# GpSimd instead of VectorE subtracts the lower parts of 24 split weight blocks in layer 3

## The chip, the cores and the metric

The kernel runs on one core of a Trainium2 chip. The metric is the device time of one execution in microseconds (us); several executions are timed and the median is taken. One further execution is recorded by the hardware profiler, and the rows below come from it. Engines are named as in the profile: PE is TensorE, PEld its weight loads, DVE is VectorE, ACT is ScalarE, POOL is GpSimd, SP is SyncE.

## The reference

The program is a trunk of four layers over 256 latent tokens and 256 context tokens, 1024 wide. Each layer has a token mixer and a squared-ReLU MLP, with a modulated input and a LayerNorm behind each. The fourth layer (number 3) mixes with a gated delta rule, and this is the layer that the change touches:

```python
def project(t):
    qkv, z, b_f, b_b, a_f, a_b = jnp.split(t @ w_in, cuts, axis=-1)
    qkv = jax.nn.silu(_centred_dwconv(qkv, conv_w))
    q, k, v = jnp.split(qkv, _cuts(GDN_KEY_DIM, GDN_KEY_DIM), axis=-1)
    q = jnp.repeat(_l2_norm(_heads(q, GDN_KEY_HEADS)), rep, axis=1) * GDN_HEAD_DIM ** -0.5
    k = jnp.repeat(_l2_norm(_heads(k, GDN_KEY_HEADS)), rep, axis=1)
    v = _heads(v, GDN_VALUE_HEADS)
...
t_inv = lax.linalg.triangular_solve(lmat, eye, left_side=True, lower=True, unit_diagonal=True)
u_vals = t_inv @ (v * beta[..., None])
...
def step(s, inp):
    u_c, w_c, q_c, a_c, k_c, d_c = inp
    v_new = u_c - w_c @ s
    o = q_c @ s + a_c @ v_new
    s = s * d_c[..., None, None] + jnp.swapaxes(k_c, -1, -2) @ v_new
    return s, o
```

There are 8 key heads and 16 value heads of 128 columns each; the sequences are cut into chunks of 64 tokens, and one triangular system is solved for each chunk and value head, in both directions.

## The kernel before

Activations lie transposed: 128 features on the partitions, tokens along the free axis. A weight block is 128 x 1024 numbers, 512 KB: 8 tiles of 128 x 128, one for each 128 of the 1024 inputs. Most products are made in three passes of a faster 32-bit format. The weight w is split into a rounded upper part `whi` and the rest `wlo = w - whi`, the activation likewise into `uh` and `ul`, and `mm3` adds three products: `ul` by `whi` (L296), `uh` by `whi` (L297), `uh` by `wlo` (L298). Queries and gates of layer 3 (`gdn_q`, `gdn_z`) are not split; they are multiplied whole in 32 bits (L1546).

For every split block `halved` does three things: SP loads it into a `raw` buffer (L271, four of them), ACT rounds it into `whi` (L279), DVE subtracts (L280) and writes `wlo`. `whi` and `wlo` have rings of four buffers. `weights` fetches two blocks ahead of the product that takes them.

Layer 3 begins in `gdn_products`. A list of jobs (`GDN_JOBS`) sets the order of the queries, keys, values and gates; beside them runs `gdn_solve`, twice, once for each group of four key heads. A key or value block gives 24 products of 512 columns in PSUM (`acc` or `pj`). Then `conv` makes a five-tap convolution: one instruction on ACT (L1389) and four on DVE (L1392), each reading the product from PSUM and the running sum `y` from SBUF. A value then goes through ACT (L233), four transposes on PE (L1587), ACT again (L1590), and POOL issues the DMA that spills it to HBM (L1591); POOL also issues the DMAs of gates (L1598) and of the solve's results (L1421, L1483).

`gdn_solve` builds its matrices on DVE from `side`, `kk` and `kq` (L1410 to L1420), transposes 32 x 32 blocks on DVE (L1441), eliminates with alternating products and differences of two SBUF tiles on DVE (L1446 and L1448), transposes back (L1452, L1453), and joins blocks by small products on PE (L1462, L1478) with copies on DVE and ACT (L1471, L1480). POOL clears tiles with memsets (L1431, L1472).

After that come the scans over chunks (`gdn_scans`), the output product and the last MLP. A scheduler lays all instructions of the program into one fixed order for each engine, from its own costs, when the program is built. Each engine works through its queue in that order, and so does SP with its DMAs.

Of the kernel before, what the change touches and what calls it, by code (L numbers as in the profile page):

```python
# [12 lines left out]
F32 = mybir.dt.float32  # L13
# [22 lines left out]
GDN_BANKS = dict(accs=3, st=3, ax=2)  # L36
GDN_PLAN = (0, 0.5, 0.4), (0, 0.6, 0.75)
GDN_JOBS = "q0 k1 q1 v v v z z z v v v z z v v z v z v v z z v v z z z z v v z v".split()
TABLES = "natural_log_exp_and_others"
GDN_ROWS = dict(y=3, x=2, v=2, side=3)  # L40
ADA_SUMS = 1
# [116 lines left out]
class Trunk:  # L158
    def __init__(self, ctx, tc, ins, out):
# [12 lines left out]
        self.wraw, self.wsplit = pool("wraw", 4), pool("wsplit", 4)  # L172
        nc.scalar.preload_act_table_set(TABLES)
        c = self.const
# [62 lines left out]
    def tables(self):  # L237

        if self.silued is not None:
            self.loaded = self.after(self.nc.scalar.preload_act_table_set(TABLES), self.silued)  # L240
            self.silued = None
# [17 lines left out]
    def load(self, name, *at):  # L259

        src = self.I[name]
        for j in at:
            src = src[j]
        if name in ("gdn_q", "gdn_z"):
            return self.whole(src)
        last = name == "mla_in" and at[0] in (4, 5) or name in ("mla_out", "diff_out", "gla_out") and at[0] >= 4 or name == "w2" and at[1] >= 4 and at[2] == 3
        return self.halved(self.tail if last else self.wsplit, src)

    def whole(self, src):
        raw = self.wraw.tile([128, 1024], F32, name="raw")  # L270
        self.nc.sync.dma_start(raw[:, :src.shape[-1]], src)  # L271
        return raw

    def halved(self, pool, src, n=""):

        nc, width = self.nc, src.shape[-1]
        raw = self.whole(src)
        hi, lo = (pool.tile([128, 1024], F32R, name=m + n) for m in ("whi", "wlo"))
        nc.scalar.copy(hi[:, :width], raw[:, :width])  # L279
        nc.vector.tensor_sub(lo[:, :width], raw[:, :width], hi[:, :width].bitcast(F32))  # L280
        return hi, lo

    def blocks(self):
# [466 lines left out]

    gdn_jobs = GDN_JOBS

# [1189 lines left out]
```

## Time and profile before

| what | value |
|---|---|
| median of 3 timed executions | 2735.97 us (2731.73 to 2740.79) |
| the profiled execution: its time | 2734.95 us |
| the profiled execution: its span | 2733.2 us |
| PE busy | 2630.0 us (96%) |
| DVE busy | 2007.7 us (73%) |
| ACT busy | 1251.6 us (46%) |
| POOL busy | 46.2 us (2%) |
| all subtractions on L280, 403 of them | 477.9 us of DVE |

The span is what the profiler's rows cover; 1.75 us of the execution's time lie around it. Busy is the time in which an engine has at least one instruction in work; for PE the ends of matmuls are modelled and run into one another, so that a busy PE isn't a PE at its peak. Layer 3's keys, values, gates and solves lie between 2007 and 2290 us of the span.

### The profile page before, as it was taken

To read this page: it belongs to the slowest core of one execution; us is meant where nothing else is said; L and a number is where in the kernel's file an instruction comes from. 1 tells how busy PE (TensorE), PEld (TensorE's weight loads), DVE (VectorE), ACT (ScalarE), POOL (GpSimd) and SP (SyncE) were. 2 spreads that over 40 slices of the span, in tenths; PEclk is the share of its full clock that TensorE was granted. 3 is DMA by queue.
4 is the path that set the end of the run, shared out by engine and by line. 5 is a ranking of instruction groups with operands and counts; after the bars stand their busy time and mean duration, and the time that the engine had idled before them with its cause. 6 is when DMAs were issued, how large, how long until landed. Compare 5 with 4: busy or idle time off the path is not lost. (4 is left out here: it accounts for less than half of the span.)

```text
span 2733.2 us, 40942 instructions
## 1 busy us (share of the span) xinstructions
PE 2630.0 (96%) x15728; PEld 2137.2 (78%) x15728; DVE 2007.7 (73%) x3796; ACT 1251.6 (46%) x2413; POOL 46.2 (2%) x71
## 2 busy tenths in 40 slices
PE   7999999999999999999999999999999998997998
PEld 5666888888866687888888897888887776667997
DVE  3577898775667798775745489876689996679666
ACT  3555453234556653333445553332464545445544
POOL 0000000000000000000000000000000111000000
PEclk9999999999999999999999999999999998999999
DMA  6533246553221137554221127654323445304453
GB/s 237 169 121 111 68 155 207 185 185 118 65 64 54 47 100 225 191 184 131 73 70 62 55 70 226 195 181 153 104 85 105 160 151 157 90 28 139 155 183 111
DMA packets 125535, 353.25 MB, mean 129 GB/s; under 512 B 37499, under 2 KB 41339, under 8 KB 124828
## 3 DMA queue, kind: packets, MB, share of 16 engines
q1 hardware_dynamic: 121804, 337.00, 38.8%
q0 software_dynamic: 3536, 13.63, 1.4%
q8 instruction: 124, 2.03, 0.3%
q14 instruction: 71, 0.58, 0.1%
HBM read 335.91 MB, written 14.68 MB: 128 GB/s over the span
## 5 line engine op out<-in xcount | busy, mean ns | idle before, releaser
L279 ACT CAST whi<-raw 128x1024 fp32r<-128x1024 f32 (+2 forms) x403 | 410.7, 1024 | 681.6 <-PE acc L297 244.9
L280 DVE TENSOR_TENSOR wlo<-raw,whi 128x1024 fp32r<-128x1024 f32 (+2 forms) x403 | 477.9, 1189 | 209.5 <-ACT whi L279 197.5
L296 PE MATMUL pj<-ul,whi 128*128 128x512 f32 (+1 forms) x1072 | 395.1, 369 | 0.1
L297 PE MATMUL pj<-uh,whi 128*128 128x512 f32 (+1 forms) x1072 | 385.2, 359 | 0.0
L298 PE MATMUL pj<-uh,wlo 128*128 128x512 f32 (+1 forms) x1072 | 383.8, 358 | 0.7 <-DVE wlo L280 0.5
L452 DVE SCALAR_TENSOR_TENSOR acc<-raw,s,acc 128x1024 f32<-128x1024 f32 x252 | 317.2, 1280 | 34.9 <-DMA raw<-in_ada 31.6
L296 PE MATMUL acc<-ul,whi 128*128 128x512 f32 (+3 forms) x888 | 312.5, 352 | 17.6 <-DVE ul L568 10.7
L297 PE MATMUL acc<-uh,whi 128*128 128x512 f32 (+3 forms) x888 | 309.8, 349 | 0.0
L298 PE MATMUL acc<-uh,wlo 128*128 128x512 f32 (+3 forms) x888 | 308.5, 348 | 0.1
L296 PEld LDWEIGHTS pj<-ul,whi 128*128 128x128 f32 x1072 | 204.0, 190 | 36.4 <-issue 6.1
L298 PEld LDWEIGHTS pj<-uh,wlo 128*128 128x128 f32 x1072 | 203.5, 190 | 34.6 <-issue 5.4
L297 PEld LDWEIGHTS pj<-uh,whi 128*128 128x128 f32 x1072 | 203.8, 190 | 29.4 <-issue 5.2
L296 PEld LDWEIGHTS acc<-ul,whi 128*128 128x128 f32 (+2 forms) x888 | 168.6, 190 | 42.3 <-DVE ul L568 12.7
L296 PE MATMUL pj<-hl,whi 128*128 128x512 f32 (+1 forms) x560 | 196.5, 351 | 1.7 <-DVE hl L635 1.3
L297 PE MATMUL acc<-hh,whi 128*128 128x512 f32 (+1 forms) x560 | 195.4, 349 | 0.0
L297 PE MATMUL pj<-hh,whi 128*128 128x512 f32 (+1 forms) x560 | 194.8, 348 | 0.0
L296 PE MATMUL acc<-hl,whi 128*128 128x512 f32 (+1 forms) x560 | 194.8, 348 | 0.0
L298 PE MATMUL acc<-hh,wlo 128*128 128x512 f32 (+1 forms) x560 | 194.7, 348 | 0.0
L298 PE MATMUL pj<-hh,wlo 128*128 128x512 f32 (+1 forms) x560 | 194.2, 347 | 0.0
L298 PEld LDWEIGHTS acc<-uh,wlo 128*128 128x128 f32 (+2 forms) x888 | 168.4, 190 | 21.8 <-issue 1.0
L297 PEld LDWEIGHTS acc<-uh,whi 128*128 128x128 f32 (+2 forms) x888 | 168.5, 190 | 20.9 <-issue 1.2
L634 ACT CAST hh<-t 128x512 fp32r<-128x512 f32 (+1 forms) x128 | 72.2, 567 | 129.7 <-DVE t L633 129.3
(463 smaller groups left out, 4887.2 us busy)
## 6 DMA issues: line engine op xcount, KB each, us to landing
raw<-in_w SPq DMA_DIRECT2D x256, 512.0 KB, 4.2
raw<-in_ada SPq DMA_DIRECT2D x192, 512.0 KB, 4.7
raw<-in_diff_qk SPq DMA_DIRECT2D x16, 512.0 KB, 3.4
raw<-in_gdn_v SPq DMA_DIRECT2D x16, 512.0 KB, 4.0
raw<-in_gdn_z SPq DMA_DIRECT2D x16, 512.0 KB, 4.0
raw<-in_gdn_out SPq DMA_DIRECT2D x16, 512.0 KB, 3.9
raw<-in_mla_in SPq DMA_DIRECT2D x9, 512.0 KB, 7.0
raw<-in_mla_qb SPq DMA_DIRECT2D x12, 384.0 KB, 3.8
```

The source lines that it names most:

```text
L279: nc.scalar.copy(hi[:, :width], raw[:, :width])
L280: nc.vector.tensor_sub(lo[:, :width], raw[:, :width], hi[:, :width].bitcast(F32))
L296: mm(ps, lhsT=ah, rhs=bl, start=start, stop=False)
L297: mm(ps, lhsT=ah, rhs=bh, start=False, stop=False)
L298: mm(ps, lhsT=al, rhs=bh, start=False, stop=stop)
L452: nc.vector.scalar_tensor_tensor(acc[r], w, self.s[:, k, r:r + 1], acc[r], op0=ALU.mult, op1=ALU.add)
L634: nc.scalar.copy(hh[:, f, :t], r[:, :t])
```

## The change

Two names are put into a table, and blocks of these names have their subtraction on POOL. `whi` stays with ACT, the DMA with SP, the arithmetic is the same.

```diff
+LOW_APART = "gdn_k", "gdn_v"
...
-        return self.halved(self.tail if last else self.wsplit, src)
+        return self.halved(self.tail if last else self.wsplit, src, low=self.nc.gpsimd if name in LOW_APART else None)
...
-    def halved(self, pool, src, n=""):
+    def halved(self, pool, src, n="", low=None):
...
-        nc.vector.tensor_sub(lo[:, :width], raw[:, :width], hi[:, :width].bitcast(F32))
+        (low or nc.vector).tensor_sub(lo[:, :width], raw[:, :width], hi[:, :width].bitcast(F32))
```

8 blocks of keys and 16 of values are concerned: 24 instructions leave DVE's queue and 24 enter POOL's. The scheduler then lays the layer out anew. After the change every line number above 38 is higher by 2.

The first place is POOL's queue where the first solve ends: `xc` and `xa` are tiles of the solve, `uc` its spilled result, `at` a spilled result of the second solve's start, `v` and `z` spilled values and gates. Before:

```order
L1598 DMA z_17226<-s 128x256
L1472 MEMSET xc 32x32x32 x2
L1472 MEMSET xa 32x32x32 x2
L1483 DMA uc_17231<-xc 128x2048
L1483 DMA uc_17233<-xa 128x2048
L1431 MEMSET xc 128x2048
L1433 MEMSET xc 128x32 x2
L1421 DMA at_17236<-side 128x512 x2
L1421 DMA at_17238<-side 128x512 x2
```

The same place of the changed kernel:

```order
L282 TENSOR_TENSOR wlo<-raw,whi 128x1024
L1474 MEMSET xc 32x32x32 x2
L1474 MEMSET xa 32x32x32 x2
L1485 DMA uc_17231<-xc 128x2048
L1600 DMA z_17226<-s 128x256
L1485 DMA uc_17233<-xa 128x2048
L1433 MEMSET xc 128x2048
L1435 MEMSET xc 128x32 x2
L282 TENSOR_TENSOR wlo<-raw,whi 128x1024
L1423 DMA at_17236<-side 128x512 x2
L282 TENSOR_TENSOR wlo<-raw,whi 128x1024
L1423 DMA at_17238<-side 128x512
```

Subtractions of value blocks now stand between POOL's memsets and spills, and start only after those ahead of them; the two first here are those of value heads 9 and 10 (counted from 0), and that of head 10 stands behind both `uc` spills and the memset of L1431.

The second place is PE's queue at the same point of the program: L1546 is a gate's product, L296 to L298 are those of a value block, L1587 transposes a value, L1462 the first joining products of the first solve. Before:

```order
L1587 MATMUL ax<-ident,x 128x128 x4
L1546 MATMUL pj<-u,raw 128x256 x2
L296 MATMUL acc<-ul,whi 128x512
L297 MATMUL acc<-uh,whi 128x512
L298 MATMUL acc<-uh,wlo 128x512
...
L296 MATMUL acc<-ul,whi 128x512
L1462 MATMUL st<-xa,lo 32x32 x64
L297 MATMUL acc<-uh,whi 128x512
```

The same place of the changed kernel:

```order
L1589 MATMUL ax<-ident,x 128x128 x4
L1548 MATMUL pj<-u,raw 128x256 x3
L1464 MATMUL st<-xa,lo 32x32 x64
L1548 MATMUL pj<-u,raw 128x256 x2
L298 MATMUL acc<-ul,whi 128x512
L1464 MATMUL st<-xa,lo 32x32 x64
L299 MATMUL acc<-uh,whi 128x512
```

Before, 34 products of value blocks (the dots leave out 30 of the same three kinds) stood between the gate's products and the first 64 joining products. Now the joining products stand ahead of these 34, so that PE reaches them earlier.

## Rows read from the trace of the kernel before

**Rows 1.** Busy time by stretch: length, then engines' busy us (instructions), PEclk, DMA share, GB/s.
```profile
1930.00:2010.00 80.00, 78.03 (x523) 71.10 (x521) 61.66 (x138) 40.42 (x79) 3.03 (x4) 1.00 0.28 88
2010.00:2085.00 75.00, 68.73 (x366) 53.15 (x367) 70.01 (x141) 40.29 (x76) 2.55 (x4) 0.98 0.33 106
2085.00:2135.00 50.00, 49.12 (x223) 40.41 (x222) 49.15 (x88) 20.52 (x49) 4.51 (x7) 0.99 0.42 135
2135.00:2210.00 75.00, 69.25 (x841) 53.76 (x840) 68.41 (x110) 46.92 (x88) 14.99 (x21) 0.98 0.44 146
2210.00:2260.00 50.00, 47.23 (x223) 39.66 (x222) 47.92 (x81) 19.50 (x47) 8.12 (x13) 1.00 0.49 157
2260.00:2285.00 25.00, 18.86 (x528) 16.66 (x528) 21.36 (x26) 17.76 (x33) 10.19 (x13) 0.71 0.62 178
```

**Rows 2.** What PE waited for, 2010 to 2285 us: total us, times, longest.
```profile
PE st L1462 <- DVE xa L1453: 4.0, 3, 1.9
PE acc L1546 <- DVE y L1392: 3.7, 1, 3.7
...
PE pj L298 <- DVE wlo L280: 0.3, 1, 0.3
```

**Rows 3.** DVE's groups by line, 2010 to 2285 us: busy us, mean ns, idle before.
```profile
L1392 DVE SCALAR_TENSOR_TENSOR y<-pj,cols,y 128x508 f32<-128x508 f32 (+3 forms) x64 | 43.6, 681 | 2.1 <-ACT y L1389 1.9
L1392 DVE SCALAR_TENSOR_TENSOR y<-acc,cols,y 128x508 f32<-128x508 f32 (+3 forms) x64 | 43.3, 678 | 5.1 <-ACT y L1389 4.9
...
L280 DVE TENSOR_TENSOR wlo<-raw,whi 128x1024 fp32r<-128x1024 f32 x24 | 29.4, 1224 | 4.4 <-ACT whi L279 4.4
...
L1452 DVE STREAM_TRANSPOSE xd<-xc 128x1024 f32<-128x1024 f32 x4 | 8.3, 2065 | 0.1
L1441 DVE STREAM_TRANSPOSE xb<-xa 128x1024 f32<-128x1024 f32 x4 | 8.0, 2044 | 1.6 <-ACT lo L1438 1.6
L1453 DVE STREAM_TRANSPOSE xa<-xc 128x1024 f32<-128x1024 f32 x4 | 7.8, 1960 | 0.0
```

**Rows 4.** DVE in order of time at four places: start us, us, instruction.
```profile
2009.42 1.23 DVE L280 TENSOR_TENSOR wlo<-raw,whi 128x1024 fp32r<-128x1024 f32 x1 [2.70 <-ACT whi L279]
...
2066.93 0.68 DVE L1436 COPY xa<-xd 32x1024 f32<-32x1024 f32 x1
...
2155.71 2.49 DVE L1471 COPY xc<-xd 32x1024 f32<-32x1024 f32 x2
2158.23 0.75 DVE L1392 SCALAR_TENSOR_TENSOR y<-acc,cols,y 128x510 f32<-128x510 f32 x1
2158.90 1.22 DVE L280 TENSOR_TENSOR wlo<-raw,whi 128x1024 fp32r<-128x1024 f32 x1
...
2162.23 1.21 DVE L280 TENSOR_TENSOR wlo<-raw,whi 128x1024 fp32r<-128x1024 f32 x1
2163.36 0.74 DVE L1392 SCALAR_TENSOR_TENSOR y<-acc,cols,y 128x508 f32<-128x508 f32 x1
```

**Rows 5.** POOL in order of time, 2155 to 2172 us.
```profile
2155.27 2.38 POOL L1472 MEMSET xc<- 32x1024 f32 x2 [11.27 <-DVE xa L1453]
2157.71 2.37 POOL L1472 MEMSET xa<- 32x1024 f32 x2
...
2170.04 1.81 POOL L1431 MEMSET xc<- 128x2048 f32 x1 [1.50 <-DMA uc<-xc]
```

**Rows 6.** POOL's memsets on 128 partitions, whole span: busy us, mean ns, idle before.
```profile
L1431 POOL MEMSET xc<- 128x2048 f32 x2 | 3.6, 1813 | 635.5 <-PE pj L298 634.0 <-DMA uc<-xc 1.5
...
L1109 POOL MEMSET ab<- 128x512 f32 x2 | 1.0, 529 | 1348.8 <-PE pj L298 1348.8
```

**Rows 7.** PE in order of time at three places: start us, us, instruction.
```profile
2010.93 0.39 PE L298 MATMUL acc<-uh,wlo 128*128 128x512 f32 x1
...
2198.99 0.63 PE L298 MATMUL pj<-uh,wlo 128*128 128x512 f32 x1
...
2222.07 0.39 PE L297 MATMUL pj<-uh,whi 128*128 128x512 f32 x1
2222.29 0.39 PE L298 MATMUL pj<-uh,wlo 128*128 128x512 f32 x1
```

## The prediction

> **What bounds the kernel now.** I read the busy time by stretch first [rows 1], because the change lies in one part of the program and the page's 73% for DVE is a mean over all of it. From 2010 to 2285 us, where the keys, values, gates and solves of layer 3 are made, DVE is busy for 256.85 of 275 us (the five stretches added), which is 93%, and in 2085 to 2135 us it has 49.15 of 50. PE shows 253.2 of 275, but its matmuls are modelled and run into one another, so that isn't a PE at its peak. In the 80 us ahead of that, the end of layer 2's MLP and the start of layer 3, it is the other way round: PE has 78.03 of 80 and DVE only 61.66. POOL has next to nothing to do in either.
>
> Then I read what PE waits for in the 275 us [rows 2]. The longest entries are DVE's results: 4.0 us for `xa` of the solve and 3.7 us for `y` of the convolution. For the subtraction itself it waits 0.3 us, once. So a subtraction isn't missed when it is late; it costs because it takes DVE's time, and whatever stands behind it in DVE's queue comes later. DVE's groups by line [rows 3] show the size: 24 subtractions in this window take 29.4 us. Four of them are of the output weights and stay; one of the concerned key blocks starts just ahead of the window, at 2009.42 us [rows 4]. That makes 21 concerned ones in this stage. The three left of the 24 that move lie in the 80 us before, where DVE has spare time and PE doesn't wait for them: I cost those at nothing. Without that cover they would cost as much apiece as the others.
>
> **What is removed.** From the start of one subtraction to that of the instruction behind it are 2163.36 - 2162.23 = 1.13 us [rows 4]. 21 of these are 23.7 us of DVE. This is the whole gift, and the upper bound of the gain.
>
> **What is added on POOL.** The trace of before has no POOL instruction that reads SBUF, so its duration is bounded from memsets [rows 6]: 128x512 takes 0.529 us and 128x2048 takes 1.813, which is 0.836 ns a column, and 0.96 us for 1024 columns of one stream. A subtraction has three streams, two that are read and one that is written. If all go side by side it takes 0.96 us, if one goes behind another 2.9. I take 1.9, the middle: two streams read one behind another, while the result is written. Both ends are kept.
>
> The Trainium skill (GPSIMD Engine Reference, section 3.1) has 4497 ns for an fp32 two-input add of 2048 columns on GpSimd; half of that, 2.25 us, would be its estimate here. With that in the place of 1.9 the sum below would come out 3.7 us later.
>
> **What it does to DVE.** Two POOL memsets of one tile run from 2155.27 us for 2.38 us, and two more from 2157.71 [rows 5]. In that time DVE's two copies of `xc` take 2.49 us; a copy of the same size without a memset beside it takes 0.68 [rows 4]. So POOL can hold up a DVE instruction. Not every one: the convolution at 2158.23 took 0.75 us and the subtraction at 2158.90 its usual 1.22 in the middle of the next memsets. A memset only writes, though. What a POOL instruction that reads two tiles does to a DVE instruction that reads two tiles, no row shows. The bounds are nothing and the whole POOL duration. I take it that they hold each other up, since the copies are the nearest row of two engines that want SBUF at once. Of the 227.4 us that DVE keeps (256.85 less 29.4), the convolutions (86.9 us) and the transposes (24.1 us) have at most one input from SBUF [rows 3]; that is 111, about half. I let this half run on, as the convolution did, and the other half be held. Each POOL subtraction then costs DVE 0.5 x 1.9 = 0.95 us and gives it 1.13, and 21 of these leave a gain of 3.8 us.
>
> **Smaller terms.** (1) The key block at 2009.42 us has no slack: its first product with `wlo` stands at 2010.93 [rows 7]. With 1.9 us it is ready at 2011.3, 0.4 us late (nothing with 0.96 us, 1.4 with 2.9). (2) Where DVE's queue held a subtraction back, POOL has it earlier; the one wait of 0.3 us for it [rows 2] goes. (3) POOL's queue: the subtraction of value head 10 now stands behind a memset that ends at 2171.9 us [rows 5], and so is done at about 2174, where DVE had it done at 2163.4 [rows 4]. Its first use is at 2198.99 [rows 7]: 25 us of cover, cost nothing. If the cover were gone the price would be those 11 us. What is queued behind it, spills of the second solve, isn't read before the scans. (4) SP's loads now wait for POOL to release a `raw` buffer; by (3) the longest such delay is 11 us, with 25 in hand.
>
> **Sum.** -23.7 + 20.0 + 0.4 - 0.3 = -3.6 us. The profiled execution took 2734.95 us, so 2731.4 of its kind; the median of before lies 1.0 above it, and I predict 2732 us. By 0.3% (8 us), about what a measurement of this kernel can tell from no change, that is no change.
>
> **Rival 1: POOL and DVE don't disturb each other (faster).** For it speaks the subtraction that ran beside a memset in its usual 1.22 us; against it the copies. The gift is then kept as far as PE can use it. In 2085 to 2135 and 2210 to 2260 us PE is busy for 96.35 of 100 us [rows 1], so the 9 subtractions there can bring 3.65 us at most. In the other stretches PE is idle for more than the 12 x 1.13 = 13.6 us that come free. The gain is 13.6 to 17.2 us; I take 14, which gives 2722 us.
>
> **Rival 2: the new order counts on time that isn't given (slower).** PE's queue has the first joining products of the solve (L1462) ahead of 34 products of value blocks that stood ahead of them. A product takes 2222.29 - 2222.07 = 0.22 to 0.23 us [rows 7], so PE arrives 34 x 0.23 = 7.8 us earlier and waits for `xa`, for which it waited already [rows 2]. If POOL's holds eat up what was freed before that point, about 14 subtractions or 15.8 us, DVE delivers no earlier, PE stands for the 7.8 us, and the convolutions behind those 34 products start late in turn. On the second solve the same shift would cost about as much again. The price is 8 to 16 us; I take 12, 2748 us. It decides from a hold of 1.13 us per POOL subtraction on: half of a duration of 2.26 us, or six tenths of 1.9. That is not far from my 0.95: the held instruction stops everything behind it in the queue, the convolutions too, so that a half is the least it can cost if holds are real.
>
> The Trainium skill (SBUF — State Buffer, section "Who interferes with whom") says that GpSimd's ports are the second pair of VectorE's, that a VectorE instruction with two SBUF inputs contends with a GpSimd instruction that reads SBUF but not with one that only writes, and that the one that comes later is blocked for the whole instruction. The rows on copies, subtraction and memsets agree with it as far as they go. By it rival 1 falls away and the case decides between the sum and rival 2.
>
> **Rival 3: nothing changes place.** The changed order has 24 subtractions on POOL, so this one is out.
>
> **How the numbers follow.** I give the sum's case 0.42, rival 1 0.34, rival 2 0.24: the holds are likelier than not, but seen on copies alone. Of the sum's case 0.05 may end faster by over 8 us and 0.01 slower; of rival 1 0.04 and of rival 2 0.02 may end within the bound. That makes 0.35 faster (0.05 + 0.30), 0.42 same (0.36 + 0.04 + 0.02) and 0.23 slower (0.22 + 0.01). The range runs from rival 1's better end, 2736 - 17 less 1 for the spread of the runs, 2718, to 2750 above rival 2's price, which with a POOL duration of 2.9 us, 21 x (1.45 - 1.13) = +6.7 us of DVE alone, is also covered. The sum's own range is 2725 to 2743.
>
> **What would show it.** POOL's rows give the duration (0.96 to 2.9 us). Holds show as DVE instructions on two SBUF tiles (L1446, L1448, L1410 to L1420) whose mean grows while L1392 keeps its 680 ns; the sum asks for about 20 us on them. Rival 1 shows unchanged means and a shorter stage, rival 2 a longer wait of L1462 for `xa`. The prediction is wrong if the holds cost much less or more than 0.95 us apiece, or if the new order moves the stage by itself.

## The result, and the profile after

The changed kernel takes 2756.28 us (median of 3, 2755.07 to 2756.57) where the kernel before takes 2735.97. The ratio is 1.0072, with a 95% interval of 1.0045 to 1.010: slower by 20 us, against a forecast of no change. In some experiments line numbers are higher by a few more than in the changed kernel.

First the busy time by stretch, in the columns of [rows 1]. The last stretch ends at 2310 us, since layer 3 ends later now:

```profile
1930.00:2010.00 80.00, 76.68 (x517) 69.45 (x516) 62.91 (x150) 38.08 (x78) 15.54 (x8) 1.00 0.23 72
2010.00:2085.00 75.00, 67.48 (x356) 51.44 (x355) 69.55 (x136) 38.76 (x75) 19.27 (x11) 0.95 0.37 115
2085.00:2135.00 50.00, 45.19 (x202) 37.34 (x201) 48.38 (x68) 18.65 (x43) 19.97 (x13) 0.97 0.40 130
2135.00:2210.00 75.00, 67.33 (x790) 50.67 (x789) 56.56 (x87) 38.60 (x67) 23.77 (x21) 0.84 0.31 110
2210.00:2260.00 50.00, 48.42 (x229) 40.41 (x227) 47.75 (x69) 22.86 (x57) 16.15 (x18) 1.00 0.50 163
2260.00:2310.00 50.00, 36.06 (x605) 30.02 (x605) 34.72 (x47) 26.37 (x52) 12.09 (x17) 0.73 0.49 145
```

DVE has lost 21 subtractions in the stage and is about as busy as before in 2010 to 2135 us (117.93 us, before 119.16). From 2135 to 2210 us it falls from 68.41 to 56.56, but PE falls too: DVE is idle there because it waits (row of L1510 below). The groups by line tell why DVE isn't freer (2010 to 2310 us; busy us, mean ns, idle before). The last row is POOL's new group, from 1930 us:

```profile
L1450 DVE TENSOR_TENSOR xc<-xc,outer 128x62 f32<-128x62 f32 (+15 forms) x62 | 45.1, 727 | 1.2
L1394 DVE SCALAR_TENSOR_TENSOR y<-pj,cols,y 128x508 f32<-128x508 f32 (+3 forms) x64 | 42.9, 672 | 1.2 <-ACT y L1391 1.0
...
L1448 DVE TENSOR_TENSOR outer<-xb,xc 128x62 f32<-128x62 f32 (+15 forms) x62 | 36.5, 588 | 1.2
...
L282 POOL TENSOR_TENSOR wlo<-raw,whi 128x1024 fp32r<-128x1024 f32 x24 | 62.4, 2605 | 688.8 <-DVE z L581 598.9 <-ACT whi L281 83.2 <-PE st L1415 5.6
```

A subtraction takes 2.6 us on POOL. The convolution (one input from SBUF) keeps its time [rows 3]; the elimination's two groups, both inputs from SBUF, are at 727 and 588 ns. The kernel before has 528 for both (2010 to 2285 us), and a run without lower parts (below) 520. First those of before, then those without lower parts:

```profile
L1448 DVE TENSOR_TENSOR xc<-xc,outer 128x62 f32<-128x62 f32 (+15 forms) x62 | 32.8, 528 | 0.9
L1446 DVE TENSOR_TENSOR outer<-xb,xc 128x62 f32<-128x62 f32 (+15 forms) x62 | 32.7, 528 | 0.8
```
```profile
L1451 DVE TENSOR_TENSOR xc<-xc,outer 128x62 f32<-128x62 f32 (+15 forms) x62 | 32.3, 520 | 1.0
L1449 DVE TENSOR_TENSOR outer<-xb,xc 128x62 f32<-128x62 f32 (+15 forms) x62 | 32.2, 520 | 1.1
```

The timelines show a single hold. First DVE, then POOL (start us, us, instruction):

```profile
2116.69 2.74 DVE L1450 TENSOR_TENSOR xc<-xc,outer 128x480 f32<-128x480 f32 x1
2119.47 0.64 DVE L1448 TENSOR_TENSOR outer<-xb,xc 128x462 f32<-128x462 f32 x1
...
2121.47 0.62 DVE L1450 TENSOR_TENSOR xc<-xc,outer 128x440 f32<-128x440 f32 x1
2122.12 2.67 DVE L1448 TENSOR_TENSOR outer<-xb,xc 128x414 f32<-128x414 f32 x1
2124.82 0.59 DVE L1450 TENSOR_TENSOR xc<-xc,outer 128x414 f32<-128x414 f32 x1
```

```profile
2116.39 2.53 POOL L282 TENSOR_TENSOR wlo<-raw,whi 128x1024 fp32r<-128x1024 f32 x1 [2.10 <-ACT whi L281]
2118.86 0.57 POOL L1600 DMA_DIRECT2D z<-s  x1
2121.58 2.75 POOL L282 TENSOR_TENSOR wlo<-raw,whi 128x1024 fp32r<-128x1024 f32 x1 [2.15 <-ACT whi L281]
```

The DVE instruction that starts inside a POOL subtraction stays until 0.5 us (about its own length) after that has ended: 2116.39 + 2.53 = 2118.92, and 2119.43 on DVE. All DVE work behind it is late by 2 us.

What PE waited for, 2010 to 2310 us, in the columns of [rows 2], and DVE's longest wait there (`issue`: the profile shows nothing that ended the wait):

```profile
PE ax L1589 <- ACT x L235: 17.0, 7, 9.6
PE acc L1548 <- issue: 6.4, 1, 6.4
PE st L1415 <- DVE side L1412: 4.5, 2, 2.5
PE st L1480 <- issue: 3.9, 1, 3.9
PE st L1464 <- DVE xa L1455: 1.4, 1, 1.4
```

```profile
DVE side L1510 <- ACT z L1561: 14.1, 3, 12.3
```

The joining products of the solve wait for `xa` for 1.4 us, before for 4.0 [rows 2]. The long wait is new: the transposes of the values (L1589), for which PE waited 2.8 us in all in the kernel before. What the 6.4 us at L1548 and the 3.9 at L1480 waited for, the profile doesn't show.

One number runs through what follows. PE's records 10,500 to 12,640 in order of time hold the same instructions in every kernel here (without lower parts they read `whi` for `wlo`; with values alone on POOL the last few differ), from the keys to the end of the second solve. I add up their durations without overlaps (busy; a lower clock makes them longer) and call the rest idle:

```
kernel                          elapsed    busy    idle   (us)
before                            278.3   256.2    22.1
before, a second profile          285.4   265.2    20.2
changed                           306.9   270.1    36.8
```

Two profiles of the kernel before agree within 2 us in idle time, but differ by 9 in busy time. Idle time is therefore what I compare.

### The profile page after: what moved, and what is told of

Same layout as the page of the kernel before. It is cut to its first block, busy times and chain, and to the rows that moved or that the text cites. A ratio compares the mean times of both kernels' runs of the same rounds, so it can differ in the third digit from the quotient of the medians.

```text
span 2754.5 us, 40962 instructions
## 1 busy us (share of the span) xinstructions
PE 2638.1 (96%) x15728; PEld 2141.5 (78%) x15728; DVE 2012.8 (73%) x3772; ACT 1250.8 (45%) x2412; POOL 109.1 (4%) x95
## 4 chain that ended last, share of the span: by engine, by line
PE 54%; DVE 11%; ACT 4%; DMA 2%; issue 1%; POOL 0%; ACTq 0%; DVEq 0%; SPq 0%
PE pj L298 8%; PE pj L299 7%; PE pj L300 7%; PE acc L298 6%; PE acc L299 6%; PE acc L300 6%; PE acc L1645 2%; DVE xc L1450 1%; DVE y L1394 1%; PE st L1670 1%; PE ax L1657 1%; DMA raw<-in_w 1%; ACT whi L281 1%; DVE outer L1448 1%; DVE wlo L282 1%
## 5 line engine op out<-in xcount | busy, mean ns | idle before, releaser
L281 ACT CAST whi<-raw 128x1024 fp32r<-128x1024 f32 (+2 forms) x403 | 410.9, 1024 | 692.9 <-PE pj L299 249.7
L282 DVE TENSOR_TENSOR wlo<-raw,whi 128x1024 fp32r<-128x1024 f32 (+1 forms) x379 | 448.7, 1187 | 208.6 <-ACT whi L281 196.9
L298 PE MATMUL pj<-ul,whi 128*128 128x512 f32 (+1 forms) x1072 | 395.8, 369 | 0.1
L298 PE MATMUL acc<-ul,whi 128*128 128x512 f32 (+3 forms) x888 | 313.2, 353 | 17.1 <-DVE ul L570 10.7
L298 PEld LDWEIGHTS pj<-ul,whi 128*128 128x128 f32 x1072 | 204.2, 190 | 36.0 <-issue 6.6
L298 PEld LDWEIGHTS acc<-ul,whi 128*128 128x128 f32 (+2 forms) x888 | 168.3, 190 | 41.8 <-DVE ul L570 12.7
L298 PE MATMUL pj<-hl,whi 128*128 128x512 f32 (+1 forms) x560 | 196.6, 351 | 1.2 <-DVE hl L637 0.8
L298 PE MATMUL acc<-hl,whi 128*128 128x512 f32 (+1 forms) x560 | 194.8, 348 | 0.0
```

What stands on the lines that cost most here:

```text
L282: (low or nc.vector).tensor_sub(lo[:, :width], raw[:, :width], hi[:, :width].bitcast(F32))
L298: mm(ps, lhsT=ah, rhs=bl, start=start, stop=False)
```

## The experiments

**Two causes, taken apart.** My theories: *holds* (POOL's reads keep DVE back for more than DVE was freed) and *order* (the layout that the scheduler made anew needs time that isn't given); the rival to both is *lateness* (`wlo` is ready later). Orders can be held fast: for PE, DVE, ACT and SP a list of the instructions of layer 3, as they stand in one kernel, is written into another, and each is tied behind the one before it in its own engine's queue. Where a run has the old order, PE's 13,460 rows stand as in the kernel before.

```diff
+def keep_order(nc, tc):
...
+    for text in ORDER:
...
+        for a, b in zip(row, row[1:]):
+            tc.add_manual_dep(ins[b], a, mybir.DependencyInfo(
+                mybir.DependencyClass.NoSync, mybir.DependencyReason.DATA), reason="order")
```

Subtractions on GpSimd, old order:

> The subtractions stand on GpSimd as in the changed kernel, but TensorE, VectorE, ScalarE and SyncE issue everything else in the order of the kernel before. If the holds cost the time (VectorE kept back by about 1.2 us per subtraction, 26 us in all, which is more than the 24 us freed), this run is about as slow as the changed kernel: 2750 to 2757 us where the kernel before takes 2736. If the new order costs it, the holds only eat what was freed: 2728 to 2740 us, no change or a little faster, and VectorE's wait at L1510 and TensorE's at L1589 are as short as before. A third reading, that GpSimd's 2.6 us make each lower part late, would show in new waits of TensorE for wlo at L299 and L300 of more than 10 us.

Subtractions on VectorE, new order:

> The subtractions stay on VectorE as in the kernel before, and the four engines issue everything else in the changed kernel's order. If the new order alone costs the time, it is slower than the kernel before by 15 us or more (2751 to 2780 us; VectorE has 24 us more to do than the order reckoned with, and no holds, which nearly cancel): L1510 and the transposes of the values wait again. If the holds cost it, this order was at least as good as the old one and the run is within 8 us of the kernel before (2728 to 2744).

Without lower parts, old order, and the same in the new order:

> Leaves out the 24 lower parts: of each such block GpSimd subtracts only 8 columns that nobody reads, and the products take the upper part in the lower one's place; the order of all else is that of the kernel before. It prices VectorE's freed time with next to no holds and no new order. Both theories: VectorE has 24 us less to do in the old order, so 2712 to 2726 us, 10 to 24 us faster. Nothing gained (over 2732) would mean that VectorE's load did not set the time of the stage at all, against the rows on which the forecast rested.

> As the run without lower parts (24 blocks subtract 8 columns, upper part in the lower one's place), but in the changed kernel's order: freed time and new order without holds. If the holds cost the time, the order is good and this comes out near the run without lower parts in the old order (within 6 us, about 2712 to 2728). If the order costs it, it is 15 us or more above that run: 2730 to 2750.

```diff
...
+        width = 8 if low else width
         (low or nc.vector).tensor_sub(lo[:, :width], raw[:, :width], hi[:, :width].bitcast(F32))
-        return hi, lo
+        return hi, hi if low else lo
```

Measured, medians, beside 2735.12 us for the kernel before in the same set; in brackets the ratio to it with its 95% interval, then the stage as above:

```
subtractions   order   us                                  elapsed    busy    idle
DVE            old     2735.12 (before)                    278.3   256.2    22.1
POOL           old     2743.04 (1.0027, 1.0015 to 1.0038)  294.0   263.6    30.4
none           old     2727.75 (0.9971, 0.9959 to 0.9984)  278.1   258.1    20.0
DVE            new     2754.86 (1.0070, 1.0055 to 1.0084)  303.5   266.3    37.2
POOL           new     2756.28 (changed)                   306.9   270.1    36.8
none           new     2734.45 (0.9998, 0.9986 to 1.0011)  282.4   263.8    18.6
```

Both causes are real. In the old order POOL costs 2743.04 - 2735.12 = 7.9 us; the new order adds 2756.28 - 2743.04 = 13.2. In the profiles the stage grows by 12.9 us from the one to the other, and 6.4 of them are idle time; the rest is busy time, by less than the two profiles of the kernel before differ. The run with POOL in the old order fell between my two ranges: each theory had a part only.

In the old order the freed time is worth little: 7.4 us with next to no hold, less than the 10 to 24 that I had expected. PE's idle time falls by 2 us at most there, so where the 7.4 us come from, the profiles don't show.

What the new order costs hangs on what else DVE and POOL have to do. Without lower parts it is 2734.45 - 2727.75 = 6.7 us, between my two ranges, and PE is idle for 18.6 us, no more than in the old one. With the subtractions on POOL it is 13.2, on DVE 19.7 (2754.86 - 2735.12, as expected of an order that costs), and PE is idle for 37. So the same 24 subtractions, left out of DVE's queue, are worth 7.4 us in the old order and 2754.86 - 2734.45 = 20.4 in the new one. Part of the 20.4 are waits: in the new order DVE stands at its subtractions for `whi` (2000 to 2310 us; before, then this run).

```profile
DVE wlo L280 <- ACT whi L279: 4.4, 4, 2.7
```
```profile
DVE wlo L280 <- ACT whi L279: 16.8, 8, 5.0
```

The transposes of the values show the difference in PE's waits (2000 to 2300 us; new order with subtractions on DVE, then without lower parts; the changed kernel has 17.0):

```profile
PE ax L1587 <- ACT x L233: 17.1, 6, 6.9
```
```profile
PE ax L1590 <- ACT x L235: 5.5, 4, 3.6
```

DVE's long wait at L1510 doesn't: it is 14.1 us in the changed kernel and 13.6 in the other two runs of the new order, the cheap one included.

Two rows of PE's waits in the run with POOL in the old order, 2000 to 2300 us, show that lateness isn't a part: `wlo` is waited for once, the transposes of the values (L1589) for 7.9 us, where the two profiles of the kernel before have 2.8 and 4.5.

```profile
PE ax L1589 <- ACT x L235: 7.9, 4, 3.7
...
PE acc L300 <- POOL wlo L282: 0.8, 1, 0.8
```

Three subtractions beside the second solve of that run (DVE, then POOL):

```profile
2240.78 0.69 DVE L1450 TENSOR_TENSOR xc<-xc,outer 128x510 f32<-128x510 f32 x1
2241.50 3.01 DVE L1448 TENSOR_TENSOR outer<-xb,xc 128x504 f32<-128x504 f32 x1
2244.55 0.68 DVE L1450 TENSOR_TENSOR xc<-xc,outer 128x504 f32<-128x504 f32 x1
2245.26 2.72 DVE L1448 TENSOR_TENSOR outer<-xb,xc 128x494 f32<-128x494 f32 x1
...
2250.79 2.85 DVE L1450 TENSOR_TENSOR xc<-xc,outer 128x462 f32<-128x462 f32 x1
```

```profile
2241.54 2.42 POOL L282 TENSOR_TENSOR wlo<-raw,whi 128x1024 fp32r<-128x1024 f32 x1
2244.80 2.66 POOL L282 TENSOR_TENSOR wlo<-raw,whi 128x1024 fp32r<-128x1024 f32 x1 [0.84 <-ACT whi L281]
...
2250.76 2.38 POOL L282 TENSOR_TENSOR wlo<-raw,whi 128x1024 fp32r<-128x1024 f32 x1 [2.27 <-ACT whi L281]
```

Each takes 2.0 to 2.3 us from DVE: 3.01 instead of 0.68, and so on. From 1930 to 2310 us 17 DVE instructions take over 0.3 us more than the longest of the same tiles and shape in the run without lower parts, and all DVE instructions together take 30.6 us longer than there (their durations added up, subtractions left out). Of this 26.6 us fall from 2010 us on.

**What holds: reading, not lateness.**

Subtracted in full, but unread:

> Old order; GpSimd subtracts the 24 blocks in full, but nobody reads the result: the products take the upper part in the lower one's place. Holds without lateness. If the 15.3 us between the run with GpSimd's subtractions in the old order (2743.0) and the run without them (2727.8) come from VectorE's holds, this run is as slow as the former: 2739 to 2746 us. If they come from the lower part being ready later (2.4 us on GpSimd against 1.2 on VectorE, behind its queue), it is as fast as the latter: 2725 to 2731.

```diff
-        return hi, lo
+        return hi, hi if low else lo
```

Lower parts left out, and the unread tile only written, behind the subtraction of 8 columns:

> Old order, lower parts left out as in the run without them, but behind each 8-column subtraction GpSimd writes zeros over the rest of the unread tile (2,032 elements of 16 bits, some 1.8 us): work of GpSimd that only writes. If GpSimd's reading of SBUF is what holds VectorE back, as the memsets of the kernel before suggested [rows 4, 5], 2725 to 2732 us and VectorE's L1450 near 530 ns again. If any access of GpSimd to SBUF does it, three quarters of the 15 us come back: 2736 to 2744 us and L1450 near 680 ns.

```diff
...
+        if low:
+            EXTRA.append(self.after(low.memset(lo[:, 8:].bitcast(mybir.dt.bfloat16), 0.0), sub))
+            return hi, hi
```

Copied, one input:

> Old order, lower parts left out (the products take the upper part in their place); GpSimd copies each upper part into the unread tile instead of subtracting: it reads one block of SBUF, not two. If holds go with the time in which GpSimd reads, whatever the number of its inputs, L1450 is above 600 ns again and the time lies between the run that only writes (2730) and the one that subtracts unread (2747), by the copy's length. If a hold needs two inputs on GpSimd as it does on VectorE, L1450 is near 525 ns and the time 2726 to 2733 us.

```diff
...
+        if low:
+            low.tensor_copy(lo[:, :width], hi[:, :width])
+            return hi, hi
```

Unread: 2747.33 us (1.0041, 1.0025 to 1.0056), idle 29.5, like the run in which PE reads the result, and just above the range for holds. Only written: 2730.07 (0.9977, 0.9968 to 0.9986), idle 19.2, in the range for reading. Copied: 2731.47 (0.9980, 0.9969 to 0.9991), idle 19.0, between the two as expected, but close to the written one. The rows of the elimination's product in the three runs, in this order, and then POOL's, show the dose (2010 to 2310 us; POOL's from 1930):

```profile
L1448 DVE TENSOR_TENSOR outer<-xb,xc 128x62 f32<-128x62 f32 (+15 forms) x62 | 44.7, 721 | 1.1
```
```profile
L1454 DVE TENSOR_TENSOR outer<-xb,xc 128x62 f32<-128x62 f32 (+15 forms) x62 | 32.5, 523 | 1.1
```
```profile
L1451 DVE TENSOR_TENSOR outer<-xb,xc 128x62 f32<-128x62 f32 (+15 forms) x62 | 35.4, 571 | 1.1
```
```profile
L282 POOL TENSOR_TENSOR wlo<-raw,whi 128x1024 fp32r<-128x1024 f32 x24 | 60.1, 2510 | 685.0 <-DVE z L581 600.9 <-ACT whi L281 79.2 <-issue 3.6
```
```profile
L287 POOL MEMSET wlo<- 128x2032 bf16 x24 | 42.9, 1787 | 0.0
```
```profile
L283 POOL CAST wlo<-whi 128x1024 fp32r<-128x1024 f32 x24 | 28.5, 1191 | 692.9 <-DVE z L584 597.8 <-ACT whi L281 95.1
```

43 us of writing leave the product at 523 ns (without any of it 520). 28.5 us of copying bring it to 571 (I had expected over 600 for the difference's group, which has 550), 60 us of subtracting to 721. So two inputs aren't needed on POOL for a hold, but it has to read. Against the run without lower parts DVE's instructions take 31.0 us longer with the unread subtraction, 8.9 with the copy and 4.5 with the write, the last mostly on copies of the solve (`xa<-xd`, `lo<-xd`), which a POOL memset holds up in [rows 4, 5] too. Lateness is out: a result that nobody waits for costs as much.

**A part of the change.** Eleven in the old order:

> The full computation in the old order, with 11 of the 24 subtractions on GpSimd: the first eight and the 17th to 19th, beside which TensorE of the run with all 24 fell no further behind the run without lower parts; the other 13 stay on VectorE. If what a subtraction costs hangs on what VectorE does beside it, these 11 cost nothing and give back part of the 7 us that the freed time is worth: 2729 to 2735 us. If each costs the same (8 us over 24), it is 2735 to 2741.

```diff
...
+        self.count = getattr(self, "count", -1) + 1
+        return self.nc.gpsimd if self.count in APART else None
```

2736.27 us against 2737.04 (1.0001, 0.9990 to 1.0013): no gain, and above the 2729 to 2735 that I had hoped for. DVE's instructions are still held for 10.3 us; I had looked for places without a hold by PE's progress, and what I found were places where PE didn't feel it. Keys alone and values alone, each in its own new order:

> The full computation with the changed kernel's edit for the 8 blocks of the keys alone, in the order that comes of it (691 of TensorE's 13,460 rows stand elsewhere than in the kernel before). Holds alone: the first eight subtractions cost nothing in the old order, so 2730 to 2738 us. If an order made anew costs whatever made it, 2743 to 2757.

> The full computation with the edit for the 16 blocks of the values alone, in the order that comes of it (845 of TensorE's rows stand elsewhere). Holds alone: 16 of 24 subtractions, and nearly all of the 8 us that they cost net in the old order: 2738 to 2745 us. Holds and order together, as in the changed kernel: 2748 to 2760.

```diff
-LOW_APART = "gdn_k", "gdn_v"
+LOW_APART = "gdn_k",
```

Keys: 2741.02 (1.0018, 1.0007 to 1.0028), between my ranges. Values: 2761.24 us (1.0095, 1.0077 to 1.0113), just above the upper one; idle 40.6. Two thirds of the subtractions cost no less than all of them (2756.28). Against the run without lower parts in the old order DVE's instructions take 27.6 us longer here and 28.9 in the changed kernel; in the old order 30.6 us of it cost 7.9. So the holds, even with the eight subtractions that DVE keeps here (9 us), hardly make the 24 us by themselves; I put the rest down to the new order.

**Whose order?** One engine's row at a time was put back, all 24 subtractions on POOL, the rest laid out by the scheduler around it.

PE:

> The full computation with the 24 subtractions on GpSimd; only TensorE issues in the order of the kernel before, the other engines as the scheduler then lays them out (298 of VectorE's 3,773 rows and 161 of ScalarE's 2,222 stand elsewhere than in the kernel before). If it is TensorE's new row, with transposes and products that wait at its head, that costs the 13 us between the changed kernel and the one in the old order, this run takes 2740 to 2747 us. If VectorE's and ScalarE's rows cost it, 2750 to 2760.

DVE:

> The full computation, 24 subtractions on GpSimd; only VectorE issues in the order of the kernel before, the others as the scheduler then lays them out (664 of TensorE's rows and 156 of ScalarE's stand elsewhere than in the kernel before). If VectorE's new row costs the order's 13 us (the convolution's sums L1394 and the elimination's updates change places, and ScalarE and TensorE wait at their heads for L1394), this run takes 2738 to 2748 us. If not, 2750 or more.

PE and DVE:

> As the run with TensorE in the old order, and VectorE in the old order too; ScalarE's row is laid out anew (141 of its 2,222 rows stand elsewhere), SyncE's comes out as before. If ScalarE's row doesn't matter, as fast as with all four in the old order: 2740 to 2747 us. If it does, 2750 or more.

ACT:

> Only ScalarE issues in the order of the kernel before; TensorE (711 rows), VectorE (288) and SyncE (48) are laid out anew. If ScalarE's row is what costs (copies of the solve ahead of the silu that the transposes wait for), 2740 to 2748 us; if VectorE's is, 2750 or more.

```
old order on       us                                  elapsed    busy    idle
all four           2743.04 (1.0027, 1.0015 to 1.0038)  294.0   263.6    30.4
PE and DVE         2757.82 (1.0077, 1.0062 to 1.0092)  302.6   268.2    34.4
DVE                2763.77 (1.0098, 1.0082 to 1.0115)  311.5   271.2    40.3
ACT                2766.22 (1.0108, 1.0093 to 1.0123)  311.7   266.8    44.9
PE                 2774.69 (1.0137, 1.0120 to 1.0154)  322.3   270.7    51.7
```

No single row is to blame: each of the three engines put back alone made the changed kernel slower, by 7 to 18 us, where its expectation asked for 8 to 18 us less. With PE, DVE and SP as before and only 141 of ACT's rows elsewhere (and four of POOL's) it costs 13 to 15 us more than with all four. There PE waits longer for the values' transposes (2000 to 2330 us), 12.6 us against 7.9 with all four rows as before:

```profile
PE ax L1589 <- ACT x L235: 12.6, 4, 4.1
```

DVE's wait for ACT's first tap of the convolution is long there too, 19.5 us against 12.5; but it is 21.0 in the run without lower parts, the fastest of all, and so explains nothing. The rows are bound to each other: a layout that keeps one and moves the others is slower than either whole one, and with PE and DVE kept it is as slow as the changed kernel. How the scheduler came to its layouts I can't see, and no run tells it.

**The kernel before once more.**

> The kernel before once more, for its profile: in the five profiles since, TensorE reached layer 3 six to ten us earlier than in the first profile of the kernel before, with the same instructions. If that is chance of one execution, TensorE's instruction 10500 starts at 1994 to 1999 us here (2004.85 in the first profile) and layer 3 takes the longer for it or the whole is shorter; if it belongs to the kernel before, at 2003 to 2006.

Record 10,500 starts at 1998.37 us: the six microseconds ahead of layer 3 were chance. The total was 2742.27 all the same, and the stage 285.4 instead of 278.3 us, with no more idle time. The stretches say where (columns as in [rows 1]):

```profile
2010.00:2085.00 75.00, 69.35 (x353) 53.68 (x354) 68.94 (x136) 40.02 (x74) 2.55 (x4) 0.93 0.30 99
2085.00:2135.00 50.00, 49.16 (x230) 40.94 (x229) 48.19 (x82) 20.69 (x51) 5.30 (x9) 1.00 0.43 135
2135.00:2210.00 75.00, 69.79 (x817) 53.75 (x816) 65.16 (x101) 43.54 (x75) 14.21 (x20) 0.89 0.43 143
```

The granted clock is 0.93 and 0.89 where the first profile had 0.98 and 0.98 [rows 1]: part of the time at 1.2 GHz, the lower of its two levels (the other is 2.4), with the same instructions; the solve's matrices and joins with their small products and waits fall into these stretches. Two profiles of one kernel differ by 7 us in this stage.

## Why the prediction was wrong

**The bound, and the gift of 23.7 us.** Mis-sized. The freed time was taken as gain in full, from DVE's 93%. Leaving the subtractions out in the old order brings 7.4 us, 0.31 of it, and PE's idle time in the stage only goes from 22.1 or 20.2 to 20.0 us. A busy share of 93% beside one of 92% for PE names no bound. In the new order the same leaving out brings 20.4 us, but from a level 19.7 above the kernel before. Rival 1 had the new order, the freed time and no holds: the run that has just that takes 2734.45 us, no change, where rival 1 asked for 2722.

The count of 21 is right by two slips that cancel: the 24 rows of the window hold the one at 2009.42 us already, and three of them, not four, are of output weights.

**POOL's duration, 1.9 us.** Mis-sized: 2.51 us in the mean in the old order, 2.61 in the new one, between the 1.9 and the upper bound of 2.9, which single ones passed (2.98, and 4.66 in the new order).

The prediction's estimate from the Trainium skill (GPSIMD Engine Reference, section 3.1), 2.25 us, was nearer, and still below the shortest one here, 2.34 us.

**The hold, 0.95 us apiece.** The mechanism was right, as was the choice of the instructions that run on (the convolution kept its 670 to 680 ns). The size was off: 30.6 / 24 = 1.28 us in the old order, 26.9 / 24 = 1.12 in the changed kernel (against the run without lower parts in the new order). I let half the work be held for the mean; in fact 17 of the 24 subtractions in the old order meet the elimination, another two-input instruction or a copy of the solve and mostly hold it until they end. With the measured sizes the sum of the 21 reads -23.7 + 26.6 = +2.9 us for the old order, where 7.9 were measured: DVE's time is not PE's time, the freed part is worth 7.4 us and the held part 15.3 (2743.04 - 2727.75). Why a held us costs more than a freed one gives, no run tells.

The Trainium skill (SBUF — State Buffer, section "Who interferes with whom") has GpSimd's reads contend with VectorE's two-input instructions and its writes not: the runs agree, 721 ns beside subtractions and 523 beside memsets. By that rule alone the forecast of a hold stood; its length comes from the rows.

**The smaller terms** hold: PE waits for a `wlo` of POOL 0.8 us in all in the old order, and the unread run shows that POOL's queue and its lateness cost nothing.

**Rival 2, the order.** This is what failed in the choice: the sum's case put the order at nothing, and rival 2 had 8 to 16 us for it with 0.24. Measured are 13.2 us. Its condition held, a hold of about 1.13 us or more. Its place didn't: L1464 waits less for `xa` than before, and the long waits stand elsewhere. That the size fits is luck in part, since it was worked out for another wait. Rows of the changed kernel show the longest case, ACT and then PE:

```profile
2265.01 0.68 ACT L1391 ACTIVATE y<-acc,cols 128x512 f32<-128x512 f32 x1
2276.09 1.04 ACT L1473 COPY xc<-xd 32x1024 f32<-32x1024 f32 x1 [10.40 <-DVE xa L1455]
2277.05 0.72 ACT L235 ACTIVATE x<-y 128x256 f32<-128x256 f32 x2
```

```profile
2277.82 1.11 PE L1589 MATMUL ax<-ident,x 128*128 128x128 f32 x4 [9.64 <-ACT x L235]
2278.86 1.92 PE L1464 MATMUL st<-xa,lo 32*32 32x32 f32 x64
```

ACT stands for 10.4 us at a copy of the solve, whose input DVE delivers late; the silu that PE's transposes need is queued behind it, and behind the transposes stand the joining products themselves. The wait of the same PE instruction in the new order is 6.9 us with the subtractions on DVE and 3.6 without lower parts; in the old order with POOL the longest at these transposes is 3.7. I priced a wait at the instruction that had moved; it came up where another engine's queue had the late result ahead of something that PE wanted.

What stays open: why this layout, and each of the partial ones, needs so much time from DVE. That the scheduler counts a POOL subtraction as shorter, or without holds, is only argued.

None of the runs with the full computation is faster than the kernel before; the best, eleven on POOL, is the same.

## What to carry to other kernels

Before work moves to GpSimd, look at whether it reads SBUF and at what VectorE does in that time: here an instruction that reads two tiles gave VectorE's two-input work holds of nearly its whole length, and 24 of 2.5 us that freed 1.13 each lost. Price freed time by leaving the work out, in the old order and in the new one, not by the engine's busy share: here the two prices were 7.4 and 20.4 us. And where a scheduler lays out the program, test an edit also in the old layout: here the layout cost more than the edit.

## What the runs showed of the hardware that was not expected

A subtraction of 128 x 1024 takes twice as long on GpSimd as on VectorE (2.51 against 1.22 us), a copy of the same size there 1.19, less than half of it. The same kernel was granted 0.93 and 0.98 of PE's clock in the same stretch of two executions, and its 29 timed runs in one set spread from 2726.77 to 2743.57 us, while the 10 of the run without lower parts in the old order stayed within 2724.46 to 2730.42.
